# Einsum of queries and keys on one core: loads issued behind a head's second copy, and the first large block loaded over all 128 partitions

## The chip, the cores and the metric

The kernel runs on one core of one Trainium2 chip. The metric is device time in microseconds (us). Runs of one kernel in one session lie within 0.5% of each other. Where two kernels are compared as a ratio, it is the mean time of one kernel's runs over that of the other's runs of the same rounds, so not quite the ratio of the medians that are quoted beside it.

## The reference

```python
batch, n_heads, seq, head_dim = 8, 12, 1024, 64      # q and k: float32
def reference(q, k):
    return np.einsum('bhid,bhjd->bhij', q, k).astype(np.float32)
```

For each of 96 heads a 1024 x 64 matrix of queries meets a 1024 x 64 matrix of keys and gives 1024 x 1024 numbers of 4 bytes. That is 50 MB to read and 403 MB to write, so storing dominates.

## The kernel before

Inputs are loaded in float32 and cast to float16 on POOL (GpSimd). DVE (VectorE) transposes them so that the 64 features lie on partitions. PE (TensorE) makes a head in four groups of four matmuls. ACT (ScalarE) copies each group from PSUM into a 4 MB tile in SBUF, and SP issues one store for each head. Heads come in blocks: blocks of 2, 2 and 4 heads first, whose inputs share a tile called early, and then eleven large blocks of 8 heads. A large block is loaded in eight pieces of 512 KB, each of 64 partitions:

```python
def pieces(self):
    parts = 2 if self.G == GMAX else 1
    return [(n, part, parts) for n in range(4) for part in range(parts)]

def load(self, piece, eng):
    n, part, parts = piece
    half, x = divmod(n, 2)                 # half block; queries or keys
    ...
    rows = slice(part * P // parts, (part + 1) * P // parts)
    eng.dma_start(out=self.raw[half][rows, x],
                  in_=src.rearrange("(p r) d -> p (r d)", p=P)[rows])
```

Six pieces of the first large block are requested at the start, in turn on SP's queue and on ACT's. All later ones are issued by ACT, behind a head's last copy:

```python
for n in range(6):
    next_load((nc.sync, nc.scalar)[n % 2])
...
        for n in range(heads):
            ...                                # transposes of the next block, as "side"
            b.scores(n, side)                  # four groups: matmuls, copy; then the store
            for _ in range(2 if b.first + n in (0, 2, 3, 4, 5) else 1):
                next_load(nc.scalar)
            to_half(i + 2 + (n == heads - 1))  # casts on POOL
```

Three 4 MB tiles take turns as output tiles (the first turn of one of them serves as early). A head's first copy therefore waits until the store of three heads ago has landed (in the trace ACT waits on stores for 311.7 us, over 91 waits). Each half block has a tile for its raw input, also three in turn. A load into one waits for POOL's casts of the half block that was there before (in the trace once, for 4.00 us).

## Time and profile before

| | before |
|---|---|
| median of 3 runs | 1079.02 us (1078.91 to 1080.22) |
| span of the profiled run | 1076.1 us |
| bytes moved | 453.28 MB, mean 421 GB/s |
| busy: PE, ACT, DVE, POOL | 65%, 65%, 40%, 33% |
| DMA engines | busy in every slice of the span |

The page and the stretches are shown in the prediction below. A stretch's last two columns are the mean busy share of the 16 DMA engines and the GB/s that they moved together.

### The profile page before, as it was taken

The page shows a single profiled execution, that of the slowest core. Times are in us where ns is not written, and L with a number is a line of the kernel's source. Part 1 is how long each engine was busy: PE and PEld are TensorE (multiplying, and loading weights), DVE is VectorE, ACT ScalarE, POOL GpSimd, SP SyncE. Part 2 cuts the span into 40 slices and gives each one's busy share as a digit, 9 for nine tenths or more (in the row PEclk, how much of TensorE's full clock was granted, in tenths as well). Part 3 has the DMA queues.
Part 4 walks back from the last instruction along what each step waited for, and adds up shares of the span by engine and source line. Part 5 has one row for each costly group of instructions (what it writes and reads, how often), then busy time and mean ns, then how long its engine had stood idle before and what let it go on. Part 6 is the DMA issues. An engine that isn't in the chain of part 4 may idle for free.

```text
span 1076.1 us, 4312 instructions
## 1 busy us (share of the span) xinstructions
PE 700.7 (65%) x1568; PEld 240.4 (22%) x1568; DVE 429.0 (40%) x57; ACT 694.5 (65%) x384; POOL 354.1 (33%) x206
## 2 busy tenths in 40 slices
PE   4866666566666757667575666757666677677770
PEld 2322222222222212222221222212222222222220
DVE  3758931910840580291094057029009307500000
ACT  2666576666656667576665766667576667678771
POOL 7578524424144141442413424135142250000000
DMA  9999999999999999999999999999999999999996
GB/s 295 425 429 429 434 429 429 428 430 426 429 421 427 427 423 427 427 427 427 425 429 420 426 425 431 429 423 435 422 426 429 430 430 434 432 432 429 432 434 290
DMA packets 22614, 453.28 MB, mean 421 GB/s; under 512 B 3136, under 2 KB 3136, under 8 KB 4672
## 3 DMA queue, kind: packets, MB, share of 16 engines
q1 hardware_dynamic: 14928, 406.33, 88.7%
q10 hardware_dynamic: 7664, 46.67, 10.7%
q8 instruction: 12, 0.20, 0.1%
q14 instruction: 10, 0.08, 0.0%
HBM read 50.33 MB, written 402.65 MB: 421 GB/s over the span
## 4 chain that ended last, share of the span: by engine, by line
DMA 73%; ACT 17%; PE 7%; DVE 1%; issue 0%; ACTq 0%
DMA out_dram<-o_sb 72%; ACT o_sb L173 16%; PE ps L162 6%; DMA early<-in_k_dram 1%; DVE o_sb L169 0%; DVE o_sb L171 0%; PE ps L143 0%; ACT o_sb L168 0%; ACTq L81 0%; ACT L168 0%; DVE kT L146 0%; DVE qT L146 0%; ACTq L173 0%
## 5 line engine op out<-in xcount | busy, mean ns | idle before, releaser
L162 PE MATMUL ps<-kT,qT 64*128 64x512 f16 x1536 | 696.8, 617 | 342.0 <-ACT o_sb L173 334.1
L173 ACT COPY o_sb<-ps 128x2048 f32<-128x2048 f32 x379 | 689.3, 1869 | 343.3 <-DMA out_dram<-o_sb 311.7
L118 POOL CAST half_sb<-x_sb 32x2048 f16<-32x2048 f32 x176 | 332.1, 1887 | 525.4 <-DMA x_sb<-in_k_dram 488.6
L162 PEld LDWEIGHTS <-qT 64*128 64x128 f16 x1536 | 237.1, 157 | 799.8 <-issue 797.5
L135 DVE STREAM_TRANSPOSE qT<-half_sb 128x2048 f16<-128x2048 f16 (+1 forms) x24 | 214.0, 8916 | 479.1 <-issue 459.3
L135 DVE STREAM_TRANSPOSE kT<-half_sb 128x2048 f16<-128x2048 f16 (+1 forms) x24 | 216.8, 9035 | 0.0
L118 POOL CAST half_sb<-early 32x1024 f16<-32x1024 f32 x16 | 16.5, 1034 | 2.4 <-DMA early<-in_k_dram 1.8
L143 PE MATMUL ps<-ident,half_sb 128*128 128x128 f16 x32 | 3.9, 309 | 8.5 <-POOL half_sb L100 5.9
L168 ACT ACT_TABLE_LOAD x1 | 1.3, 1283 | 12.4 <-DMA early<-in_k_dram 12.4
L169 DVE COPY o_sb<-ps 128x1024 f32<-128x1024 f32 x4 | 4.8, 1222 | 7.8 <-ACT o_sb L168 7.8
L100 POOL CAST half_sb<-early 128x512 f16<-128x512 f32 x8 | 4.7, 616 | 4.1 <-DMA early<-in_q_dram 3.9
L168 ACT COPY o_sb<-ps 128x1024 f32<-128x1024 f32 x4 | 4.0, 1014 | 3.0 <-PE ps L162 3.0
L146 DVE COPY qT<-ps 128x1024 f16<-128x1024 f16 x2 | 2.5, 1225 | 8.0 <-PE ps L143 8.0
L143 PEld LDWEIGHTS <-half_sb 128*128 128x128 f16 x32 | 3.3, 142 | 10.1 <-POOL half_sb L100 5.9
L146 DVE COPY kT<-ps 128x1024 f16<-128x1024 f16 x2 | 2.4, 1220 | 4.9 <-PE ps L143 4.9
L171 DVE COPY o_sb<-ps 128x2048 f32<-128x2048 f32 x1 | 2.3, 2291 | 2.0 <-PE ps L162 2.0
masks.py:199 POOL TENSOR_SCALAR_AFFINE_SELECT ident<-ident 128x128 f16<-128x128 f16 x1 | 0.3, 293 | 0.1
masks.py:197 POOL MEMSET ident<- 128x128 f16 x1 | 0.2, 205 | 0.3 <-POOLq L276 0.3
L276 POOL MEMSET const-float32-0.0<- 128x1 f32 x1 | 0.1, 98 | 0.2 <-issue 0.2
L276 POOL MEMSET const-bfloat16-1.0<- 128x1 bf16 x1 | 0.1, 101 | 0.0
L276 POOL MEMSET const-uint8-127<- 128x1 uint8 x1 | 0.1, 101 | 0.0
L276 POOL MEMSET const-float32-1.0<- 128x1 f32 x1 | 0.1, 98 | 0.0
## 6 DMA issues: line engine op xcount, KB each, us to landing
out_dram<-o_sb SPq DMA_DIRECT2D x96, 4096.0 KB, 25.6
x_sb<-in_k_dram ACTq DMA_DIRECT2D x43, 512.0 KB, 12.4
x_sb<-in_q_dram ACTq DMA_DIRECT2D x42, 512.0 KB, 12.5
early<-in_q_dram SPq DMA_DIRECT2D x4, 256.0 KB, 4.9
early<-in_k_dram ACTq DMA_DIRECT2D x4, 256.0 KB, 5.3
early<-in_q_dram SPq DMA_DIRECT2D x2, 512.0 KB, 8.7
early<-in_k_dram ACTq DMA_DIRECT2D x2, 512.0 KB, 9.2
x_sb<-in_q_dram SPq DMA_DIRECT2D x2, 512.0 KB, 13.0
```

What stands on the lines that cost most here:

```text
L100: nc.gpsimd.tensor_copy(out=self.halves[x][:, :, half], in_=self.raw[half][:, x].rearrange("p (r d) -> p r d", d=D),)
L118: nc.gpsimd.tensor_copy(out=dst[:, :, b % 2], in_=raw[32 * b : 32 * b + 32, :, :, h],)
L135: pin(nc.vector.transpose(out=dst, in_=src))
L143: pin(nc.tensor.transpose(t_ps[:, t], self.halves[x][:, t], ident))
L146: pin(nc.vector.tensor_copy(out=dst, in_=src))
L162: nc.tensor.matmul(ps[:, tt, js], qT[cs, g, 2 * u + tt], kT[cs, g, js])
L168: pin(nc.scalar.copy(out=dst[:, 0], in_=ps[:, 0]))
L169: pin(nc.vector.tensor_copy(out=dst[:, 1], in_=ps[:, 1]))
L171: pin(nc.vector.tensor_copy(out=dst, in_=ps))
L173: pin(nc.scalar.copy(out=dst, in_=ps))
L276: nc = _bacc.Bacc("TRN2", target_bir_lowering=False, num_devices=1)
```

## The change

The change does two things. The first large block comes in four pieces of 1 MB over all 128 partitions, three of them requested at the start. And each load is issued behind the second of a head's four copies, so that it is requested earlier in the head.

```diff
-            parts = 2 if self.G == GMAX else 1
+            parts = 2 if self.first > 2 * GMAX else 1
...
-                if u in side:
-                    side[u]()
+                for do in side.get(u, []):
+                    do()
...
-    for n in range(6):
+    for n in range(3):
         next_load((nc.sync, nc.scalar)[n % 2])
...
+            loads = 2 if 2 <= b.first + n < 6 else 1
+            side[1] = side.get(1, []) + [lambda: next_load(nc.scalar)] * loads
             b.scores(n, side)
-            for _ in range(2 if b.first + n in (0, 2, 3, 4, 5) else 1):
-                next_load(nc.scalar)
             to_half(i + 2 + (n == heads - 1))
```

More of the change, by code (lines that the diff above doesn't have):

```diff
@@ L252 @@
                 if n == 1:
-                    side = {u: lambda x=u // 2: nxt.transpose_rows(x) for u in (1, 3)}
+                    side = {
+                        u: [lambda x=u // 2: nxt.transpose_rows(x)] for u in (1, 3)
+                    }
             elif nxt:
@@ L256 @@
                 some = [s for m, s in enumerate(parts) if m * heads // 4 == n]
-                side = {0: lambda: [nxt.transpose_quads(*s) for s in some]}
+                side = {0: [lambda s=s: nxt.transpose_quads(*s) for s in some]}
+            loads = 2 if 2 <= b.first + n < 6 else 1
+            side[1] = side.get(1, []) + [lambda: next_load(nc.scalar)] * loads
             b.scores(n, side)
-            for _ in range(2 if b.first + n in (0, 2, 3, 4, 5) else 1):
-                next_load(nc.scalar)
             to_half(i + 2 + (n == heads - 1))
```

## The prediction

> **What bounds the kernel now.** I read the page first (the busy table in slices, the DMA queues, the chain), then stretches of the trace, then the timeline of ACT and of the DMA issues in the first 75 us.
>
> ```profile
> DMA  9999999999999999999999999999999999999996
> GB/s 295 425 429 429 434 429 429 428 430 426 429 421 427 427 423 427 427 427 427 425 429 420 426 425 431 429 423 435 422 426 429 430 430 434 432 432 429 432 434 290
> DMA packets 22614, 453.28 MB, mean 421 GB/s; under 512 B 3136, under 2 KB 3136, under 8 KB 4672
> ...
> DMA out_dram<-o_sb 72%; ACT o_sb L173 16%; PE ps L162 6%; DMA early<-in_k_dram 1%; DVE o_sb L169 0%; DVE o_sb L171 0%; PE ps L143 0%; ACT o_sb L168 0%; ACTq L81 0%; ACT L168 0%; DVE kT L146 0%; DVE qT L146 0%; ACTq L173 0%
> ```
>
> The DMA engines are busy in every slice and move about 428 GB/s in all slices but the first and the last. The bytes are fixed: 453.28 MB / 428 GB/s = 1059 us. The span is 1076.1 us, so about 17 us are lost at the two ends. ACT and PE, 65% busy each, mostly wait for the stores. The stretches say where the 17 us are (columns: stretch, length, busy time and count of PE, weight loads, DVE, ACT, POOL, clock, DMA share, GB/s):
>
> ```profile
> 0.00:12.00 12.00, 4.55 (x23) 2.86 (x24) 2.35 (x2) 0.00 (x0) 5.50 (x15) 1.00 0.86 321
> 12.00:28.00 16.00, 9.05 (x27) 3.37 (x26) 7.90 (x6) 7.11 (x6) 15.38 (x15) 1.00 1.07 293
> 28.00:34.00 6.00, 4.58 (x16) 1.96 (x15) 1.08 (x2) 3.63 (x2) 1.68 (x3) 1.00 0.93 401
> 34.00:100.00 66.00, 47.22 (x104) 15.79 (x105) 51.46 (x9) 43.68 (x25) 47.95 (x26) 1.00 1.00 428
> 100.00:870.00 770.00, 501.02 (x1104) 170.75 (x1104) 329.91 (x37) 503.39 (x277) 272.21 (x145) 1.00 1.00 427
> 870.00:1040.00 170.00, 125.49 (x277) 42.86 (x277) 36.34 (x4) 125.95 (x71) 11.34 (x6) 1.00 1.00 431
> 1040.00:1064.00 24.00, 8.82 (x20) 2.84 (x18) 0.00 (x0) 10.73 (x6) 0.00 (x0) 1.00 1.01 434
> 1064.00:1076.10 12.10, 0.00 (x0) 0.00 (x0) 0.00 (x0) 0.00 (x0) 0.00 (x0) 1.00 0.28 120
> ```
>
> Lost against 428 GB/s: 12 x (1 - 321/428) = 3.0 us up to 12 us; 16 x (1 - 293/428) = 5.0 us from 12 to 28; 6 x (1 - 401/428) = 0.4 us to 34; nothing to speak of up to 1064; and 12.1 x (1 - 120/428) = 8.7 us at the end. Together 17.1 us, which closes the account. The change can only touch the middle of these: between 12 and 28 us the engines are busy (share 1.07) and yet slow. Narrower stretches:
>
> ```profile
> 12.00:13.00 1.00, 0.91 (x3) 0.18 (x2) 0.00 (x0) 0.64 (x1) 0.96 (x2) 1.00 1.21 434
> 13.00:14.00 1.00, 0.00 (x0) 0.00 (x0) 0.00 (x0) 0.99 (x2) 0.99 (x1) 1.00 1.01 221
> ...
> 18.00:19.00 1.00, 1.00 (x4) 0.33 (x2) 0.08 (x1) 0.89 (x1) 0.96 (x2) 1.00 0.98 270
> ...
> 25.00:26.00 1.00, 0.00 (x0) 0.00 (x0) 1.00 (x1) 0.00 (x0) 0.96 (x2) 1.00 1.03 221
> ```
>
> Up to 13 us it is the loads into the tile early, 128 partitions each: 434 GB/s. Then only the first large block's loads are left, eight of 64 partitions and 512 KB, and the rate is about 270 GB/s while both queues carry them (half the pieces on SP, rows 0 to 63, the others on ACT, rows 64 to 127). At 24 to 26 us the ACT queue has nearly all of the traffic and the rate is 221 to 238 GB/s.
>
> [...]
>
> **The change, part by part.**
>
> *Whole loads.* The first large block now comes in four pieces of 1 MB over 128 partitions. Its 4.19 MB take 4.19 / 0.270 = 15.5 us at the present rate (the trace has them from about 13 to 28 us). At 420 GB/s, a little under the 434 of the early loads, they take 10.0 us. What is saved is engine time, and engine time is the bound here as long as there is something else to move: 5.5 us at most. Some of the slow stretch was shared with the first store, so I use the 5.0 us lost from 12 to 28 and leave 0.3 us of it for whole loads running at 420: 4.7 us saved, plus the 0.4 us to 34.
>
> *Does the next work arrive in time?* If the loads end early and the first store is late, the engines idle and the gain is gone. The ACT timeline and the issues on SP:
>
> ```profile
> 11.86 0.47 ACTq L81 DMA_DIRECT2D x_sb<-in_q_dram  x1
> 12.36 1.28 ACT L168 ACT_TABLE_LOAD   x1 [12.36 <-DMA early<-in_k_dram]
> 13.66 1.93 ACT L168 COPY o_sb<-ps 128x1024 f32<-128x1024 f32 x2
> ...
> 55.09 0.47 ACTq L81 DMA_DIRECT2D x_sb<-in_q_dram  x1
> 55.74 3.63 ACT L173 COPY o_sb<-ps 128x2048 f32<-128x2048 f32 x2 [4.00 <-POOL half_sb L118]
> ```
>
> Today ACT issues three loads before its table load, and the third waits until 11.86 us for an early load to land. So the first copy starts at 13.66 although its matmuls, begun at 9.34 with 1.9 us for four, were done at 11.25. In the order of the changed kernel ACT has one load there (8.10 us is when the like of it went today): table load 8.6 to 9.9, first copy at 11.25, 2.4 us earlier. All of the first heads is a chain of copies, matmuls and transposes without a DMA, so the stores, issued today at 21.88, 34.03, 44.12, 51.76 and 63.22 us, move to 19.5, 31.6 and 41.7 for the first three. Supply against demand, at 427 GB/s after 3.1 us lost: early 4.19 and block three 4.19 MB are moved at 22.7 us (store 0 is there since 19.5); with store 0 and one more load, 13.1 MB, at 33.8 (store 1 at 31.6); with store 1 and two loads 18.4 MB, at 46.1 (store 2 at 41.7); with store 2 and two loads 23.6 MB, at 58.4. No gap up to there.
>
> *Loads behind the second copy.* This removes no instruction; one load goes from 0.47 us of issue after copy four to 0.47 us beside copy two, which takes 1.87 us. The price is a load whose buffer is not yet free: it now stops ACT in the middle of a head. The only such wait today is the 4.00 us at 51.7 to 55.7 above, at the end of head three. The buffer is freed by POOL's casts of the first half block, which start again at 43.53 us when the transposes release a tile; six more of 1.93 us end at 55.1. With the chain 2.4 us earlier they end at 52.7. In the changed kernel that load stands behind head three's second copy, at 45.6 us: ACT stops for about 7.1 us, then makes two copies, and store 3 goes at 57.1 instead of 51.8. The engines have work until 58.4, so this fits with 1 us to spare; I charge 0.5 us for unequal engines. Head five's wait on the second half block (casts end at 68) comes when ACT gets there, at about 68, and costs nothing. Later, ACT waits on stores for 311.7 us over 91 waits, and POOL waits for loads 488.6 us, so buffers are free long before.
>
> Sum: 4.7 + 0.4 - 0.5 - 0.2 for small gaps = 4.4 us. 1079.0 - 4.4 = 1074.6 us.
>
> **Rivals.** (a) The slow rate comes from the 8 KB rows and not from the 64 partitions. Against it: one half alone runs at half of 434[...]; for it: the early loads have rows of 2 and 4 KB, so no whole load with 8 KB rows is in this trace. Then loads stay near 270 and about 0.5 us is left: 1078.5. (b) The stop in head three is longer, or the engines drain sooner, and a new gap of 2 to 4 us near 55 us takes half or more of the gain: 1077 to 1078. The margin of 1 us is my weakest number. (c) The loads' new place shifts the mix of loads and stores in the steady state. From 34 to 1064 us the rate matters: 0.2% of it is 2 us, in either direction: 1072.5 to 1076.5. (d) No gain because the stores are hidden anyway: against it, engine share is 1.00 throughout, so each saved microsecond of engine time at the start must show at the end.
>
> **Range and chances.** Full gain with no new gap is 5.1 us (1073.9); rival (c) can add 1.5 us to that; (a) or (b) leave 0.5 to 2 us. The three runs of before span 1.3 us. So 1072.3 to 1078.2. The 2% threshold is 21.6 us, more than all that is lost at both ends; nothing in the change can reach it.
>
> **What would show it.** Right: between 13 and 22 us some 420 GB/s; the table load at about 8.6 us and the first copy at 11.25; first store issued at 19.5; a stop of ACT of about 7 us on POOL in head three at 45.6; 428 GB/s from 28 us on; the last 12 us as today. Wrong: 270 GB/s still at 18 us (rival a), a stretch near 55 us under 400 GB/s (rival b), or a steady state other than 427 to 428 (rival c).

The sum is 4.7 + 0.4 - 0.5 - 0.2 = 4.4 us, so 1079.0 - 4.4 = 1074.6 us. The first two terms are estimates worked out from the stretches above (293 and 401 GB/s against 428, and 434 for the early loads). The 0.5 and the 0.2 us are allowances of mine that no measured number gives.

## The result

The changed kernel took 1068.64 us (median of 4 runs, 1067.64 to 1069.56) against 1079.37 us for the kernel before in the same rounds. The ratio is 0.990 with a 95% interval of 0.9882 to 0.9917. It is faster by 10.7 us, where I had forecast 4.4 us and a lowest time of 1072.3 us. So the prediction was wrong.

The slices of the changed kernel (GB/s in 40 equal parts of the span) differ from those before mainly at the two ends: 381 for 295 in the first, 323 for 290 in the last.

```profile
GB/s 381 430 420 429 432 425 434 427 423 434 427 428 427 424 431 422 427 426 428 432 419 428 429 430 427 423 431 430 430 427 425 431 431 432 431 432 431 431 431 323
```

The stretches of the changed kernel, with the columns of the prediction:

```profile
0.00:12.00 12.00, 4.62 (x23) 2.88 (x24) 2.36 (x2) 2.12 (x2) 5.60 (x15) 1.00 0.87 331
12.00:28.00 16.00, 13.08 (x40) 5.09 (x39) 8.32 (x6) 7.53 (x7) 15.34 (x15) 1.00 1.04 426
28.00:34.00 6.00, 4.39 (x14) 1.70 (x12) 5.48 (x3) 3.38 (x3) 4.81 (x3) 1.00 1.03 441
34.00:100.00 66.00, 45.40 (x101) 15.10 (x100) 49.52 (x8) 45.30 (x26) 49.43 (x27) 1.00 1.00 424
100.00:870.00 770.00, 505.12 (x1114) 172.44 (x1113) 326.98 (x36) 505.22 (x278) 274.94 (x146) 1.00 1.00 428
...
1040.00:1064.00 24.00, 3.17 (x8) 0.88 (x6) 0.00 (x0) 4.89 (x3) 0.00 (x0) 1.00 0.88 380
1064.00:1067.80 3.80, 0.00 (x0) 0.00 (x0) 0.00 (x0) 0.00 (x0) 0.00 (x0) 1.00 0.03 11
```

Held against 428 GB/s, as in the prediction, the stretch from 12 to 34 us loses 16 x (1 - 426/428) + 6 x (1 - 441/428) = -0.1 us, where it lost 5.4. That is the forecast gain. But two more places gave something that was not forecast. From 1040 us to the end the loss is 24 x (1 - 380/428) + 3.8 x (1 - 11/428) = 6.4 us; before it was 24 x (1 - 434/428) + 12.1 x (1 - 120/428) = 8.4 us, so 2.0 us less. And from 100 to 870 us the rate is 428 for 427 GB/s, 1.8 us (1.3 us when the bytes of the trace's packets are summed, since the view prints whole numbers). The stretch from 34 to 100 us gave back 0.6 us. The profiled pair differs by 8.3 us (1076.1 against 1067.8), less than the medians' 10.7, because the profiled run of before was a quick one (1077.89 us) and that of the changed kernel a slow one (1069.56 us).

What the prediction said of the first 55 us came out well. ACT's timeline in the changed kernel:

```profile
8.28 0.33 ACTq L81 DMA_DIRECT2D x_sb<-in_k_dram  x1
8.65 1.28 ACT L168 ACT_TABLE_LOAD   x1 [8.65 <-DMA early<-in_k_dram]
11.16 1.01 ACT L168 COPY o_sb<-ps 128x1024 f32<-128x1024 f32 x1 [1.24 <-PE ps L162]
...
50.34 0.47 ACTq L81 DMA_DIRECT2D x_sb<-in_q_dram  x1
50.86 3.63 ACT L173 COPY o_sb<-ps 128x2048 f32<-128x2048 f32 x2 [7.77 <-POOL half_sb L118]
```

The first copy starts at 11.16 us (forecast 11.25), and the stop on POOL in head three is 7.77 us (forecast about 7.1). The first four stores as SP issues them, first in the kernel before and then in the changed one (start, duration):

```profile
21.88 0.36 SPq L177 DMA_DIRECT2D out_dram<-o_sb  x1
34.03 0.35 SPq L177 DMA_DIRECT2D out_dram<-o_sb  x1
44.12 0.33 SPq L177 DMA_DIRECT2D out_dram<-o_sb  x1
51.76 0.33 SPq L177 DMA_DIRECT2D out_dram<-o_sb  x1
```

```profile
19.39 0.35 SPq L177 DMA_DIRECT2D out_dram<-o_sb  x1
29.21 0.34 SPq L177 DMA_DIRECT2D out_dram<-o_sb  x1
39.28 0.33 SPq L177 DMA_DIRECT2D out_dram<-o_sb  x1
54.52 0.33 SPq L177 DMA_DIRECT2D out_dram<-o_sb  x1
```

**One more reading of the same traces.** The rate is a mean over 16 engines. The trace records every increment of a transfer's completion semaphore, and there are sixteen for each transfer (3136 for the 196 transfers of the kernel before). In the last store they can be held against the packets of 32 KB that are under way at the same moment, worked out from the trace records. In the kernel before there are 16 of them at 1063.85 us, 1 us before the first increment. Then their number falls as the increments come: 8 packets at 1066.85 us with 8 increments still to come, 5 with 5 at 1069.85 and 1 with 1 at 1073.85. In the changed kernel it is 16 packets at 1058.59 us, 5 with 5 increments to come at 1062.59 and 2 with 2 at 1064.59. So I read each increment as the end of one engine's part of the store, though it does not say which engine it is. The profiled span ends 1.5 us after the last increment in the kernel before and 1.3 us after it in the changed one. The sixteen in order, in us after the first of them, worked out from the trace records:

```
before          0.0 0.1 0.5 0.7 0.8 1.1 1.6 1.9 2.9 4.1 4.2 6.4 6.9 7.6 8.3  9.8
changed kernel  0.0 0.6 0.7 0.7 0.8 0.9 1.0 1.8 2.0 2.8 3.0 4.0 4.3 4.6 5.8  6.9
```

The time when the median engine (the mean of the eighth and ninth) ends its part of the last store, and when the last engine does:

| | median engine | last engine | lag |
|---|---|---|---|
| before | 1067.2 us | 1074.6 us | 7.4 us |
| changed kernel | 1061.5 us | 1066.5 us | 5.0 us |

The median engine gained 5.7 us, close to the 5.1 us that the prediction gave as the full gain. Another 2.4 us came from a smaller lag of the slowest engine. I had taken that tail for fixed. These are single profiles, though: in k0_again below, the same changed kernel once more, the median engine ends at 1059.4 us and the lag is 5.4 us, so the time of the median engine varies by some 2 us from one execution to the next.

### The profile page after: what moved, and what is told of

It is laid out like the page before. It is cut to its first block, busy times and chain, and to the rows that moved or that the text cites. A ratio compares the mean times of both kernels' runs of the same rounds, so it can differ in the third digit from the quotient of the medians.

```text
span 1067.8 us, 4308 instructions
## 1 busy us (share of the span) xinstructions
PE 700.8 (66%) x1568; PEld 240.8 (23%) x1568; DVE 429.0 (40%) x57; ACT 694.4 (65%) x384; POOL 354.5 (33%) x206
## 3 DMA queue, kind: packets, MB, share of 16 engines
q10 hardware_dynamic: 7552, 46.14, 10.4%
## 4 chain that ended last, share of the span: by engine, by line
DMA 70%; ACT 17%; PE 7%; DVE 1%; POOL 1%; issue 1%; ACTq 0%; SPq 0%; POOLq 0%
DMA out_dram<-o_sb 70%; ACT o_sb L173 17%; PE ps L162 7%; POOL half_sb L118 1%; DVE kT L135 0%; DMA early<-in_q_dram 0%; DVE o_sb L169 0%; DVE kT L146 0%; DVE o_sb L171 0%; PE ps L143 0%; ACT o_sb L168 0%; ACTq L81 0%; DVE qT L146 0%; ACTq L173 0%; POOL half_sb L100 0%
```

## The experiments

Two theories stood against each other. In theory A all of the gain is the loads of 64 partitions at the start, counted by the slowest engine. In theory B the earlier issue in the head is worth several microseconds by itself in the steady state. Ten kernels ran. Each was timed over five rounds beside the kernel before, whose medians were 1078.65, 1079.23 and 1079.05 us in the three sessions. Differences below are taken within a session where not said otherwise. Diffs are against the changed kernel where not said otherwise.

### k0_again: the changed kernel as the yardstick

No edit.

> The changed kernel once more, as the yardstick for the others of this call. The first measurement gave 1068.6 us against 1079.4, 10.7 us where I had forecast 4.4. If that holds: 1067.5 to 1069.6. Its trace should again show the last transfers ending within about 7 us of each other (the stretch with a falling rate at the end), against about 10 us before.

Measured: 1068.0 us (1067.37 to 1068.32) against 1078.65, ratio interval 0.9886 to 0.9914. The gain of 10.7 us stands. The median engine ends at 1059.4 us, the last one 5.4 us after it.

### e1_whole_only: whole loads, issue behind the last copy

```diff
-            side[1] = side.get(1, []) + [lambda: next_load(nc.scalar)] * loads
             b.scores(n, side)
+            for _ in range(loads):
+                next_load(nc.scalar)
```

> Whole loads for the first large block, every load behind the last copy as before. Theory A ([...]it counts by the slowest of the 16 DMA engines and not by the mean rate, so that it also shows in the shorter tail): within 1.5 us of the changed kernel, 1068 to 1070. Theory B (the earlier issue in the head is worth some 5 us in the steady state): 1073 to 1075. The ACT stop on POOL should be back behind head three's last copy.

Measured: 1073.57 us (1071.95 to 1075.59), ratio interval 0.9944 to 0.9973. That is 5.1 us for the whole loads alone, what the prediction had meant for the whole change. Theory A falls: 5.6 us are missing against k0_again. The start of its trace is as good as that of the changed kernel from 12 to 28 us (columns as before):

```profile
12.00:28.00 16.00, 12.31 (x35) 4.55 (x33) 8.41 (x6) 6.51 (x6) 15.33 (x16) 1.00 1.05 442
28.00:34.00 6.00, 4.43 (x17) 2.02 (x16) 4.11 (x2) 3.38 (x3) 4.12 (x3) 1.00 0.91 340
```

Its median engine ends at 1062.0 us, against 1061.5 and 1059.4 in the two traces of the changed kernel. The last one ends 6.8 us later, at 1068.9. (The profiled run, 1071.95 us, is the fastest of the six.)

### e2_move_only: issue behind the second copy, the first large block in pieces of 64 partitions

```diff
-            parts = 2 if self.first > 2 * GMAX else 1
+            parts = 2 if self.G == GMAX else 1
-    for n in range(3):
+    for n in range(6):
-            loads = 2 if 2 <= b.first + n < 6 else 1
+            loads = 2 if b.first + n in (0, 2, 3, 4, 5) else 1
```

> The loads issued behind the second copy, the first large block in pieces of 64 partitions as before. Theory A: 1077.5 to 1079.5, with 270 GB/s from 13 us on and the long tail. Theory B: 1073 to 1075.

Measured: 1074.63 us (1072.87 to 1076.8), ratio interval 0.995 to 0.9977. So moving the issue alone gives 4.0 us, in the range that theory B gave.

```profile
12.00:28.00 16.00, 11.52 (x33) 4.46 (x32) 8.22 (x6) 7.42 (x7) 15.33 (x16) 1.00 1.07 274
...
100.00:870.00 770.00, 501.09 (x1104) 170.75 (x1104) 327.02 (x37) 503.58 (x278) 269.55 (x144) 1.00 1.00 428
```

The slow stretch at the start is still there (274 GB/s). The median engine ends at 1067.2 us, as before, and the lag is 4.5 us where it was 7.4. In these traces whole loads go with an earlier median engine and the place of the issue with a smaller lag. The split is not clean: of the 4.1 us between the profiles of e1_whole_only and k0_again (spans 1070.2 and 1066.1) 2.6 are in the median engine and some 1.5 in the lag. Alone the two halves give 5.1 + 4.0 = 9.1 of the 10.7 us.

### e3_all_columns: every piece over 128 partitions

Later pieces are cut by columns and not by rows, so that each spans all partitions with rows of 4 KB.

```diff
-            rows = slice(part * P // parts, (part + 1) * P // parts)
+            w = self.elems // parts
+            cols = slice(part * w, (part + 1) * w)
-                    out=self.raw[half][rows, x],
-                    in_=src.rearrange("(p r) d -> p (r d)", p=P)[rows],
+                    out=self.raw[half][:, x, cols],
+                    in_=src.rearrange("(p r) d -> p (r d)", p=P)[:, cols],
```

> The changed kernel, but every later piece of 512 KB spans all 128 partitions, cut by columns (rows of 4 KB) and not by rows. Same bytes, same number of loads. Theory A says that loads of 64 partitions load the engines unequally all through the kernel: then the tail shrinks below the 6.4 us lost of the changed kernel and the time falls to 1063 to 1067. If the tail comes from something else: 1068 to 1069. [...]

Cut is a third case, over 1069 us, whose condition no run shows.

Measured: 1067.59 us (1066.92 to 1067.73), ratio interval 0.9882 to 0.991, which overlaps that of k0_again. The forecast of a shorter tail was a miss, and an instructive one:

```profile
100.00:870.00 770.00, 502.45 (x1108) 171.07 (x1106) 326.74 (x36) 502.42 (x277) 270.08 (x144) 1.00 1.01 431
...
1040.00:1064.00 24.00, 1.23 (x3) 0.16 (x1) 0.00 (x0) 3.13 (x2) 0.00 (x0) 1.00 0.61 262
```

The mean rate from 100 to 870 us rose from 428 to 431 GB/s, worth 770 x 3/428 = 5.4 us. Nearly all of that was lost again from 1040 us on. The ends of the engines in the last store, as above, from the trace records:

```
k0_again        0.0 0.3 0.6 0.6 1.2 1.4 1.8 1.9 2.1 2.9 3.4 4.0 4.2 4.3 5.2  7.3
e1_whole_only   0.0 0.3 0.6 0.6 0.7 1.9 2.0 2.0 3.5 4.2 5.2 6.2 7.2 7.6 8.1  9.6
e2_move_only    0.0 0.2 0.7 0.9 0.9 1.2 1.4 1.6 2.7 2.9 3.5 3.6 4.0 4.2 5.4  6.6
e3_all_columns  0.0 0.0 0.0 0.0 0.1 0.1 0.1 0.1 0.1 0.3 1.0 1.3 2.0 2.2 2.4 10.6
```

With loads of 64 partitions the engines end all over the last 7 to 10 us. In e3_all_columns fifteen of them end within 2.4 us, and a single one comes 8.2 us later. Its lag grows steadily, by about 0.1 us in each store, to 10.5 us after 96 of them. So the median engine is done at 1054.2 us, 7.3 and 5.2 us before that of the two traces of the changed kernel, but the last one ends at 1064.7 us, against 1066.5 and 1064.8 in the two traces of the changed kernel. The end follows the slowest engine and not the mean. The edit does two things at once: each piece spans 128 partitions, and its rows are half as long (4 KB for 8).

### e4_columns_last: the same, behind the last copy

e3_all_columns with the edit of e1_whole_only.

> All loads over 128 partitions (cut by columns, as in e3_all_columns) but issued behind the last copy. In the runs so far the end is set by the slowest of the 16 DMA engines, and the place of the issue changed how far it lags behind the median: 7.4 and 6.8 us with the last copy, 5.0, 5.4 and 4.5 us with the second. If the place matters only because loads of 64 partitions disturb the engines unequally, this run equals e3_all_columns: 1067 to 1068.5, lag again near 10.5 us of one engine alone. If the place matters by itself: 1070 to 1072.

Measured: 1068.33 us (1067.02 to 1068.6), ratio interval 0.9887 to 0.9914; the slowest engine lags at the end by 10.4 us against the median, as in e3_all_columns, with one other at 6.3 us. (They ran in two sessions on two chips, each beside the kernel before.) The last place costs 5.6 us with row-cut pieces. With column-cut ones the gains over the kernel before are 11.1 and 10.9 us, with intervals of some 1.5 us either way. So it is no cost of ACT, and not of the queue as such: it goes with the row-cut pieces. Whether it is their 64 partitions or their 8 KB rows, no run separates.

### e5_first_copy and e9_third_copy: other places

```diff
-            side[1] = side.get(1, []) + [lambda: next_load(nc.scalar)] * loads
+            side[0] = side.get(0, []) + [lambda: next_load(nc.scalar)] * loads   # e9: side[2]
```

> The changed kernel with loads behind the first copy in place of the second. If earlier is better by degrees (4 us for two copies): 1065 to 1067. If the gain of the place comes only from being away from the store's issue: 1067.5 to 1069.5, as the changed kernel. The stop on POOL in head three comes one copy earlier, which should cost under 1 us.

Measured: 1069.43 us (1068.22 to 1069.67), ratio interval 0.9898 to 0.9925. The lag is 4.8 us. This is no test of an earlier place, though, as the two traces show (k0_again first, then this run):

```profile
406.37 1.87 ACT L173 COPY o_sb<-ps 128x2048 f32<-128x2048 f32 x1 [3.82 <-DMA out_dram<-o_sb]
406.42 0.47 ACTq L81 DMA_DIRECT2D x_sb<-in_k_dram  x1
```

```profile
409.31 1.87 ACT L173 COPY o_sb<-ps 128x2048 f32<-128x2048 f32 x1 [3.71 <-DMA out_dram<-o_sb]
409.33 0.47 ACTq L81 DMA_DIRECT2D x_sb<-in_k_dram  x1
```

In both, the load goes out as the head's first copy starts, whether it is written behind the first copy or the second. From 150 to 840 us a load is issued 7.4 us ahead of the next store in both kernels (median, worked out from the trace records). So this run serves as one more repeat of the changed kernel.

> The changed kernel with loads behind the third copy. So far: last copy 1073.6, second 1068.0, first 1069.4 us (each beside its own runs of before at 1078.7 to 1079.2). If only the last place is bad, where the load's issue falls within 2 us of the store's issue: 1067.5 to 1069.5. If the cost grows with each copy: 1070 to 1071.5.

Measured: 1071.62 us (1070.95 to 1073.14), ratio interval 0.9919 to 0.9947, with a lag of 8.2 us. Here a load is issued 3.7 us ahead of the next store, in e1_whole_only 1.9 us. The cost therefore begins with the third copy.

### e6_last_store_15: taking work from one engine

From e3_all_columns, the last store in two parts, of 8 and of 120 rows.

```diff
+            last = self.first + n == BH - 1
+            for part in (slice(120, 128), slice(0, 120)) if last else (slice(0, P),):
                 nc.sync.dma_start(out=...[part], in_=...[part])
```

> As e3_all_columns, but the last store is split into 8 rows and 120 rows[...]. If the one engine that lags by 10.5 us is the sixteenth: its 9.7 us of the last store fall away, 1057.5 to 1060. If it is another one: 1067.5 to 1069[...].

Cut is which engines take which rows, an assumption of mine that no run shows. The first case stands for: the engine that lags has nothing to do in the last store. The 9.7 us are 4.19 MB at the 431 GB/s of the stores; that they would fall away was my estimate.

Measured: 1075.53 us (1074.73 to 1077.42), ratio interval 0.9962 to 0.9987. It is slower than both of my cases, a miss. In the records the slowest engine of the store before the last ends at 1059.8 us. The last increment of the 8-row part comes at 1062.0 us and the 120-row part ends at 1071.6, 9.6 us after that. The 120-row transfer was slow in itself, for a reason that no run shows: its fifteen increments, where an undivided store has sixteen, spread from 1056.5 to 1071.6 us. The records do not say which rows an engine takes, so this run does not settle which engine it is.

### e7_no_stop: no stop of ACT in head three

```diff
-            loads = 2 if 2 <= b.first + n < 6 else 1
+            loads = 2 if b.first + n in (2, 4, 5, 6) else 1
```

> The changed kernel with head three taking one load and head six two, so that no load waits for POOL in the middle of head three. My prediction charged 0.5 us for that stop; the trace shows a dip to 287 GB/s at 56 to 58 us, worth 0.7 us. If that counts at the end: 1067.0 to 1068.0 against 1068.0 to 1068.6 for the changed kernel. If the slowest engine does not feel it: no difference.

Measured: 1069.01 us (1067.01 to 1069.45), ratio interval 0.9887 to 0.9914, the same as k0_again. The dip is less deep, first the changed kernel and then this one:

```profile
56.00:58.00 2.00, 1.77 (x5) 0.59 (x4) 0.00 (x0) 2.00 (x2) 1.96 (x2) 1.00 0.84 287
```

```profile
56.00:58.00 2.00, 2.00 (x6) 0.79 (x5) 0.00 (x0) 0.49 (x1) 1.96 (x2) 1.00 0.89 373
```

Nothing of that is seen at the end, within the some 1.5 us that these rounds resolve.

### e10_before_columns: the kernel before with one edit

The column cut of e3_all_columns put into the kernel before, and nothing else.

> The kernel before with one edit: each 512 KB piece spans 128 partitions, cut by columns; loads stay behind the last copy, and ACT still issues three loads ahead of its table load, so the first store stays near 21.9 us. If loads of 64 partitions are the whole matter, and the place and the earlier first store count for nothing beside them: 1067.5 to 1069.5, the stretch from 12 to 28 us near 420 GB/s. If the earlier first store (19.4 us in the changed kernel) is worth its 2.5 us at the end: 1070 to 1071.5. If the gain needs the place as well: 1072 to 1075.

Measured: 1068.86 us (1068.36 to 1070.4), ratio interval 0.9895 to 0.9923. One edit that moves no issue gives 10.2 us, as much as the whole change within the interval.

```profile
12.00:28.00 16.00, 11.05 (x32) 4.06 (x30) 8.32 (x6) 6.71 (x6) 15.33 (x16) 1.00 1.06 420
...
100.00:870.00 770.00, 508.24 (x1120) 173.53 (x1120) 327.34 (x37) 508.65 (x281) 266.79 (x142) 1.00 1.01 431
```

Its first store is issued at 21.12 us and not at 19.39, so the earlier first store is not needed. What the edit does to a load is seen in the time from its issue to its landing (last number, median in us), in the kernel before and then here:

```profile
x_sb<-in_k_dram ACTq DMA_DIRECT2D x43, 512.0 KB, 12.4
x_sb<-in_k_dram ACTq DMA_DIRECT2D x43, 512.0 KB, 24.8
```

Each column-cut load takes twice as long to land, and the kernel is faster all the same. So the edit also changes how long a load takes beside the stores (24.8 us for 12.4), and whether that comes from the shorter rows is not shown. No run has pieces of 128 partitions with rows of 8 KB in the later blocks, or of 64 with rows of 4 KB, so what of the gain beyond the first 34 us is the partitions' and what the rows' is not shown. No version beat the changed kernel beyond doubt: e3_all_columns has a median lower by 0.4 us, with overlapping intervals.

## Why the prediction was wrong

- **Bound and account.** That the DMA engines are the bound held. That the account closes at 17 us held too, but the sentence drawn from it, "The change can only touch the middle of these", is the step that failed. The account is one of the mean over engines. The last 8.7 us were not a fixed cost of finishing. They were the time in which some engines had finished and others had not; the DMA share of 0.28 in the prediction's line for 1064 to 1076 us had room for that, and the share was not "1.00 throughout", as rival (d) says.
- **Whole loads.** Right that they are faster (426 GB/s from 12 to 28 us for 293), nearly right in size: 4.7 + 0.4 us forecast for the loads, 5.1 us measured in e1_whole_only, 5.7 us for the median engine. Rival (a), the 8 KB rows as the cause, is refuted: the changed kernel has whole loads with 8 KB rows and moves 426 GB/s from 12 to 28 us. Two slips did not matter. SP had three of the eight pieces and not half (its queue issued three), so ACT's queue carried both halves at the end, one after the other (its loads issued at 11.86, 19.59 and 20.10 us had their last increments at 27.17, 32.40 and 39.71). And the range ends at 1078.2 us, below rival (a)'s own 1078.5.
- **Does the next work arrive in time.** The first copy and the first store came within 0.1 us of the forecast. Stores 1 to 3 came 2.4 to 2.6 us earlier than forecast (29.21, 39.28 and 54.52 against 31.6, 41.7 and 57.1), so the margin was larger than I feared. e10_before_columns shows that the earlier first store was not needed.
- **Loads behind the second copy.** This is where the missing microseconds lie, and here too a step failed: I gave this part only a price (0.5 us for the stop) and no gain. That there was none to expect was an assumption of mine and not shown by any trace. The mean rate from 100 to 870 us did stay nearly the same (428 for 427 GB/s in e2_move_only), but the end came 4.0 us earlier. The stop is about as long as forecast, but e7_no_stop shows no gain from removing it. The move alone is worth 4.0 us (e2_move_only), and 5.6 us beside whole loads (k0_again against e1_whole_only). In the profiled pairs it shows as a smaller lag of the slowest engine: 7.4 to 4.5 us without whole loads, 6.8 to 5.0 and 5.4 us with them. That is 1.4 to 2.9 us, less than the medians give, so the lag is part of the answer and not shown to be all of it.
- **Rival (c)** named the right part and the right direction, "the loads' new place shifts the mix of loads and stores", and gave 1072.5 us at best. I counted it as a mean rate only, and it was too small.
- **Rivals (b) and (d).** The sign set for (b), under 400 GB/s near 55 us, did appear (287 GB/s from 56 to 58 us), but it was worth 0.7 us and e7_no_stop shows no loss from it. What was saved at the start did show at the end, so (d) fell as forecast.

What the runs show about the move's cause is this. The cost of the late issue goes with the row-cut pieces (e4_columns_last against e3_all_columns). It is there when a load is issued 1.9 or 3.7 us ahead of the next store and gone at 7.4 us. It goes in part with the lag of the slowest engine: 6.8 to 8.2 us in the three traces with row-cut pieces and a late issue (before, e1_whole_only, e9_third_copy), 4.4 to 5.4 us in the five with an early one. In the four kernels of the two-part comparison, whose later loads are row-cut, the engines end over 6.6 to 9.8 us. With column-cut loads fifteen of them end within 2.4 and 3.3 us (e3_all_columns, e10_before_columns), fourteen within 1.6 us (e4_columns_last), and the last at 8.9 to 10.6 us. What makes the row-cut pieces special, their 64 partitions or their longer rows, no run shows. Why the lag that goes with them depends on the place in the head stays open. The records do not say which increment belongs to which engine, so no run here can show it.

## What to carry to other kernels

When DMA engines are busy throughout, count the slowest engine and not the mean rate: here a falling rate in the last microseconds was engines finishing one after another (in the kernel before 16 packets under way at 1063.85 us, 1 at 1073.85), and edits far from the end changed it. Try large loads cut so that each still spans all 128 partitions; here one such edit, which also halved the rows and moved no issue, was worth 10.2 us. Test the halves of a two-part change apart before explaining it, because here each half alone gave about half of the gain. And look in the trace whether an edit moved what it was to move: in e5_first_copy it did not.
